# The opening's modulation as rows on TensorE in four column tiles, and the queries' rotation in two parts, in a two-layer retention, attention and gated-linear-attention block on one Trainium2 core

## The chip, the cores and the metric

One core of one Trainium2 chip runs the whole kernel. The metric is device time in microseconds (us), lower is better. Before the change the median of three runs is 1180.37 us (1178.66 to 1183.4). Engines are called as the profile calls them: PE (TensorE, with PEld for its weight loads), DVE (VectorE), ACT (ScalarE), POOL (GpSimd), SP (SyncE, which issues the DMAs). Names like L556 are line numbers of the kernel before.

## The reference, cut to what matters

```python
c_act = jax.nn.silu(c)
for l in range(2):                                    # DEPTH
    shift, scale, gate = split(c_act @ ada_w[l] + ada_b[l], 3)     # 1024 x 3072
    h = rms_norm(x, norm_w[l]) * (1 + scale) + shift
    proj = h @ w_in[l]
    # retention: rope(rq), rope(rk), rv, gate rz; 4 heads of 64, chunks of 64
    # mla: 8 heads, q = (rms_norm(q_lat) @ w_uq), 64 plain + 32 rotated columns
    #      k, v from kv_lat, masked softmax by chunks of 64
    # gla: 4 heads, gated linear attention
    mixed = concat(r_o * silu(rz), m_o * silu(mz), g_o * silu(gz))
    x = x + gate * (mixed @ w_out[l])
return rms_norm(x, final_norm)                        # x is 1024 x 1024, fp32
```

All is fp32. A product of two fp32 tiles is made by `mm3` (L556 to L558): both operands are split into a high and a low part of the type fp32r, and hi·hi, hi·lo and lo·hi are added in PSUM, so three matmuls for each pair of 128 x 128 weights and 512 tokens. A plain fp32 matmul shows as two passes in the trace.

## The kernel before, in words

The tokens lie along the free dimension, in two halves (hf) of 512; features lie on partitions, in eight tiles (KT = 8, index k) of 128. The order of instructions on each engine is the order of the program text. Beside the main stream of projections runs a list of tasks: Python generators that `tick()` advances. Each `yield n` in a task means "continue n ticks later", and a tick comes after each group of three matmuls of a projection. So a `yield` decides between which of the projections' matmuls a task's instructions stand on each engine.

**The opening** (`start`). The norm of x and the modulation of layer 0 must be there before the first projections. Shift and scale are columns of `ada_w[0]` times silu(c), 8 tiles of 128 columns each. `column(k)` makes tile k of both: the scale's on DVE (L301, a product with a replicated row of silu(c), summed along the free dimension), the shift's for k = 0 to 4 (SHIFT_PE = 5) on PE by eight fp32 matmuls of one column (L311), for k = 5 to 7 on DVE as well. `make(k)` then forms h of tile k for both halves: DVE `ht` (L347), ACT high part (L348, with the shift as its bias), DVE low part (L354). Between the second and the third stands `column(k + 1)`. The first three weights, rq1, rq2 and rk1 (their tiles are named ssq_wh, ada_wh and mkh_wh in the trace), are split into high and low by ACT (L456) and DVE (L457): the first ahead, the others after `make(0)` and `make(1)`. The table `behind` gives PE one weight's matmuls after `make(0)`, three groups after `make(1)` and five after `make(2)`; from k = 3 on all three weights' (18 matmuls). After k = 2 ACT makes the sines of the positions (`trig`, L406 to L410, with two loads of its table).

**The queries** (`mla_queries`). The rotated columns of the queries are made first: two tiles for each half (`qx`). After a tick, `q_rope` rotates both halves on DVE (L732 to L737, six operations of 128 x 512 each), splits them (cast on DVE L1118, rest on POOL L1119) and writes them to DRAM (qr). Then come eight tiles of the plain columns (four pairs of heads by two halves, trace name mq_pspj, 6 matmuls each), each emptied by `pair_out`: ACT high part L1106, DVE low part L1107, two writes. They go through two PSUM banks ("pj"). Retention's blocks run as a task beside this: scores (L790), DVE's masked scores `ram` (L793) and weighted keys `rks` (L804), the state (L802, L815, `rst` L825), values (L830, L834), then a norm (`hsq` L860 on ACT, its sum L862 on DVE).

**The maxima** (`mla_max`). Ahead of the softmax each head's scores are made once in one pass only to find row maxima: 12 units for each head, a matmul of 128 to 512 keys (L1243) and DVE's maximum (L1245), one unit per 1.15 ticks. q (qn and qr) and k are read back from DRAM. When a head's units are done, its close reduces (L1211), waits `yield 4`, and transposes the maxima on PE (L1215). The close of head h stands inside head h + 1, ahead of its third group of queries, and it is run inside the same generator, so its yield also moves all later units. Units that are left when the values' projection (mv, L1189) comes up are issued back to back ahead of it.

## Time and profile before

| what | value |
|---|---|
| median of three runs | 1180.37 us (1178.66 to 1183.4) |
| the profiled execution | 1183.94 us, its span 1182.2 us |
| mean granted clock of PE in it | 0.978 |
| PE / DVE / ACT / POOL busy | 95% / 66% / 50% / 44% of the span |
| DMA | 169.01 MB, mean 143 GB/s |

The span is the time from the first to the last instruction in the profiled execution, and all rows of the trace are placed in it by their start. A row of the timeline reads: start, duration, engine, line, operation, output<-inputs, shape, number of instructions put together, and in brackets how long the engine had been idle and what ended that. Durations of matmuls are modelled and overlap: the time of one in a dense stretch is the distance between two starts. In the table of windows each engine's busy time stands with the number of its instructions, then the granted clock (1.00 is full), the share of the DMA engines and their GB/s.

### The profile page before, as it was taken

How to read it: one execution, taken by the hardware profiler on the slowest of the kernel's cores; microseconds unless marked ns; L12 is line 12 of the kernel's file. 1: busy time of each engine (PE TensorE's matmuls, PEld its weight loads, DVE VectorE, ACT ScalarE, POOL GpSimd, SP SyncE). 2: the span in 40 equal slices, each digit the busy share in tenths (PEclk: the TensorE clock that was granted, in tenths of full speed). 3: DMA queues.
4: the chain of work that ended last, by engine and by line, in shares of the span. 5: the costliest groups of instructions: out<-in, count | busy, mean ns of one | idle time of the engine just before them, and what ended most of it. 6: DMA issues, size and time to landing. Idle time of an engine off the chain costs nothing.

```text
span 1182.2 us, 16973 instructions
## 1 busy us (share of the span) xinstructions
PE 1118.6 (95%) x5968; PEld 933.9 (79%) x5968; DVE 785.9 (66%) x1366; ACT 596.2 (50%) x1164; POOL 525.8 (44%) x459
## 2 busy tenths in 40 slices
PE   6999996899999999999999999969999999999996
PEld 3878985688878788887787898748888878888896
DVE  6866666568765656868875476474866565686754
ACT  6434342243554678863543434324355557886431
POOL 0055152445433446683565333335453344668620
PEclk8899998899999999999999999989999999999999
DMA  9725661662137534238443356155211653424722
GB/s 370 257 87 161 203 223 54 213 194 73 41 96 216 130 90 108 64 134 311 178 167 101 113 169 239 38 213 150 63 59 41 199 130 90 108 63 156 255 88 72
DMA packets 65585, 169.01 MB, mean 143 GB/s; under 512 B 10262, under 2 KB 13334, under 8 KB 65500
## 3 DMA queue, kind: packets, MB, share of 16 engines
q1 hardware_dynamic: 65500, 167.93, 44.8%
q8 instruction: 47, 0.77, 0.3%
q14 instruction: 38, 0.31, 0.1%
HBM read 125.36 MB, written 38.41 MB: 139 GB/s over the span
## 4 chain that ended last, share of the span: by engine, by line
PE 75%; DVE 12%; DMA 5%; ACT 4%; issue 3%; POOL 1%; SPq 0%; DVEq 0%; POOLq 0%; ACTq 0%
PE mhead_psacc L1294 3%; PE mhead_psacc L1292 3%; PE mhead_psacc L1293 3%; PE pmz_pspj L556 3%; PE pmz_pspj L557 2%; PE pmz_pspj L558 2%; DMA ada_aw<-awc 2%; DVE mmax_mx L1245 2%; PE wo_pss L558 2%; PE wo_pspj L556 2%; PE wo_pss L556 2%; PE wo_pss L557 2%; PE wo_pspj L558 2%; PE wo_pspj L557 2%; PE mhead_pss L1260 2%
## 5 line engine op out<-in xcount | busy, mean ns | idle before, releaser
L457 POOL TENSOR_TENSOR wwo_wl<-wwo_wst,wwo_wh 128x1024 fp32r<-128x1024 f32 x27 | 69.4, 2575 | 39.0 <-ACT wwo_wh L456 38.9
L1245 DVE TENSOR_REDUCE mmax_mx<-mmax_psmm 128x1 f32<-128x512 f32 (+1 forms) x96 | 57.4, 598 | 34.9 <-PE mmax_psmm L1243 33.9
L1269 POOL TENSOR_TENSOR mhead_wh<-mhead_p,mhead_wh 128x384 fp32r<-128x384 f32 (+1 forms) x48 | 57.9, 1207 | 45.5 <-DVE mhead_wh L1268 39.9
L576 DVE SCALAR_TENSOR_TENSOR ada_aw<-ada_aw,silrow 128x512 f32<-128x512 f32 x64 | 60.6, 966 | 18.6 <-DMA ada_aw<-awc 18.4
L1274 DVE TENSOR_TENSOR mhead_ph<-mhead_pss,mhead_ph 128x512 fp32r<-128x512 f32 x48 | 33.0, 688 | 36.2 <-ACT mhead_pss L1273 35.7
L556 PE MATMUL pmz_pspj<-mkh_h,wmz_wh 128*128 128x512 f32 x128 | 53.3, 417 | 0.0
L1269 POOL TENSOR_TENSOR mhead_wl<-mhead_p,mhead_wl 128x128 fp32r<-128x128 f32 (+1 forms) x48 | 35.8, 746 | 34.7 <-DVE mhead_wl L1268 34.7
L557 PE MATMUL pmz_pspj<-mkh_h,wmz_wh 128*128 128x512 f32 x128 | 50.9, 397 | 0.0
L558 PE MATMUL pmz_pspj<-mkh_h,wmz_wl 128*128 128x512 f32 x128 | 50.6, 395 | 0.0
L556 PE MATMUL mq_pspj<-latn_lat,wuq_wh 128*128 128x512 f32 x48 | 21.6, 450 | 26.0 <-DVE mq_pl L1107 25.6
L558 PE MATMUL wo_pspj<-gran_mx,wwo_wl 128*128 128x512 f32 (+1 forms) x120 | 44.3, 369 | 1.9 <-POOL wwo_wl L457 1.9
L556 PE MATMUL wo_pss<-gran_mx,wwo_wh 128*128 128x512 f32 (+1 forms) x120 | 44.5, 371 | 0.0
L556 PE MATMUL wo_pspj<-gran_mx,wwo_wh 128*128 128x512 f32 (+1 forms) x120 | 44.5, 371 | 0.0
L557 PE MATMUL wo_pss<-gran_mx,wwo_wh 128*128 128x512 f32 (+1 forms) x120 | 44.1, 368 | 0.0
L557 PE MATMUL wo_pspj<-gran_mx,wwo_wh 128*128 128x512 f32 (+1 forms) x120 | 44.1, 368 | 0.0
L558 PE MATMUL wo_pss<-gran_mx,wwo_wl 128*128 128x512 f32 (+1 forms) x120 | 44.1, 368 | 0.0
L457 POOL TENSOR_TENSOR wrk_wl<-wrk_wst,wrk_wh 128x1024 fp32r<-128x1024 f32 x3 | 8.0, 2682 | 79.5 <-ACT wrk_wh L456 79.5
L600 ACT ACTIVATE ssq_sq<-ssq_x 128x512 f32<-128x512 f32 (+1 forms) x31 | 16.6, 534 | 50.9 <-DVE ssq_x L1371 50.9
L605 DVE TENSOR_TENSOR ssq_sq<-ssq_sq,ssq_sq 128x512 f32<-128x512 f32 (+1 forms) x30 | 30.9, 1029 | 13.6 <-ACT ssq_sq L600 13.6
L1272 ACT ACTIVATE mhead_ph<-mhead_pss 128x512 fp32r<-128x512 f32 x48 | 28.6, 596 | 17.8 <-PE mhead_pss L1262 17.3
L1243 PE MATMUL mmax_psmm<-mmax_mxk,mmax_mxq 104*128 104x512 f32 (+1 forms) x96 | 35.5, 370 | 2.0 <-DVE mmax_mx L1245 1.5
L556 PE MATMUL pv_pspj<-wgv_wh,mkh_h 128*128 128x256 f32 x128 | 37.0, 289 | 0.0
(560 smaller groups left out, 4124.7 us busy)
## 6 DMA issues: line engine op xcount, KB each, us to landing
ada_aw<-awc SPq DMA_DIRECT2D x64, 256.0 KB
wwo_wst<-wo SPq DMA_DIRECT2D x32, 512.0 KB
aw<-awc SPq DMA_DIRECT2D x11, 512.0 KB
x<-xT SPq DMA_DIRECT2D x8, 512.0 KB
kn<-mk_ph SPq DMA_DIRECT2D x16, 256.0 KB
kn<-mk_pl SPq DMA_DIRECT2D x16, 256.0 KB
qn<-mq_ph SPq DMA_DIRECT2D x16, 256.0 KB
qn<-mq_pl SPq DMA_DIRECT2D x16, 256.0 KB
```

Source lines behind the costliest of these rows:

```text
L457: (eng or nc.gpsimd).tensor_tensor(lo, src, hi.bitcast(F32), ALU.subtract)
L556: mm(ps, lh, rh, start=start, stop=False)
L557: mm(ps, lh, rl, start=False, stop=False)
L558: self.last = mm(ps, ll, rh, start=False, stop=stop)
L576: step = nc.vector.scalar_tensor_tensor(v, v, 1.0, self.silrow[:, cs], ALU.mult, ALU.mult, accum_out=t[:, 2 * j + i:2 * j + i + 1])
L1243: nc.tensor.matmul(ps[:, :w], st["q"][0:104, 128 * i:128 * i + 128], st["k"][0:104, 512 * j:512 * j + w], start=True, stop=True)
L1245: nc.vector.tensor_reduce(mx[:, i, j:j + 1], ps[:, :w], AX.X, ALU.max)
L1269: nc.gpsimd.tensor_tensor(pl, p, ph.bitcast(F32), ALU.subtract)
L1274: nc.vector.tensor_tensor(pl, s, ph.bitcast(F32), ALU.subtract)
L1292: mm(acc[:, o], vh, ph, start=(j == 0), stop=False, skip_group_check=True)
L1293: mm(acc[0:64, o], vl, ph, start=False, stop=False, skip_group_check=True)
L1294: mm(acc[:, o], vh, pl, start=False, stop=last, skip_group_check=True)
```

## The change

It has four parts.

1. **The opening's first half as columns, its second half as rows.** Columns 0 to 3 stay with `column(k)`: shift of k = 0 on PE, all other sums on DVE. Columns 4 to 7 of shift and scale are made as two rows of 512 on PE: `row(1)` after k = 1 and `row(3)` after k = 2. Each is eight fp32 matmuls of 32 x 512 with silu(c), repeated 32 times, as the stationary operand, four at a time in the four column tiles of the array (`tile_position` (0, 32j)), which leaves four partial sums at 32 partitions each. ACT copies the bank, and after rq1's matmuls of the next k `row_out` turns the row into four columns: four matmuls of one column with a selector that adds the four partial sums, and DVE writes them into `mod` (`ada_out`). The weights' loads and splits for all three names come ahead of the columns; `behind` is gone, so each k does its 18 matmuls at once; `trig` stands after k = 3.
2. **The queries' rotation** of half 0 stands right behind that half's two tiles, that of half 1 behind the eight plain tiles.
3. **`yield 4` in the maxima's close is `yield 7`.**
4. Two inputs are laid out for the rows (`awk`, a 0/1 selector column `sel`). The bytes loaded in the opening stay sixteen tiles of 512 KB.

```diff
-SHIFT_PE = 5
...
-    A["aws"] = ada_w[0][:, :128 * SHIFT_PE].reshape(KT, 128, SHIFT_PE, 128).transpose(2, 1, 0, 3).reshape(SHIFT_PE, 128, D)
+    A["aws"] = ada_w[0][:, :128].reshape(KT, 128, 128).transpose(1, 0, 2).reshape(128, D)
+    A["awk"] = ada_w[0].reshape(4, 2, 128, 6, 512)[:, :, :, 1:4:2].transpose(3, 0, 2, 1, 4).reshape(2, 4, 128, 1024)
...
                 dma(pos, A["pos"])
         names = ("rq1", "rq2", "rk1")
         wst, aw = {}, {}
-        for k in range(KT):
-            if k < len(names):
-                wst[names[k]] = self.sl(name="wst")
-                dma(wst[names[k]], A["wi"][0, MIDX[names[k]]])
+        for n in names:
+            wst[n] = self.sl(name="wst")
+            dma(wst[n], A["wi"][0, MIDX[n]])
+        for k in range(4):
             aw[k] = [self.sl(name="aw") for _ in range(2)]
-            dma(aw[k][1], A["awc"][2 + k // 4, k % 4])
-            dma(aw[k][0], A["aws"][k] if k < SHIFT_PE else A["awc"][k // 4, k % 4])
+            dma(aw[k][1], A["awc"][2, k])
+            dma(aw[k][0], A["awc"][0, k] if k else A["aws"])
+        for ch in (1, 3):
+            aw["row", ch] = [self.sl(name="aw") for _ in range(4)]
+            for i in range(4):
+                dma(aw["row", ch][i], A["awk"][ch // 2, i])
         self.ahead()
         V.memset(self.ones, 1.0)
         V.memset(self.eps, EPS)
...
         ssq = [self.ps("acc") for _ in range(2)]
         o = VO["c"]
         self.silu(self.silc, self.vec[:, o:o + KT], self.sm([128, KT]), self.sm([128, KT]))
+        silrep = self.pt((128, KT, 32), name="silrep")
+        V.tensor_copy(silrep, self.silc.unsqueeze(2).to_broadcast([128, KT, 32]))
         ab = self.sm([128, KT])
         o = VO["adab"]
         V.tensor_scalar(ab, self.vec[:, o + KT:o + 2 * KT], 1.0, None, ALU.add)
...
             V.scalar_tensor_tensor(self.mod[0][2 + ch][:, j], t[:, 1:2], ab[:, k:k + 1], self.vec[:, o:o + 1],
                                    ALU.add, ALU.mult)
             src = t[:, 0:1]
-            if k < SHIFT_PE:
+            if k == 0:
                 ps = self.ps()
                 for i in range(KT):
                     nc.tensor.matmul(ps[:, 0:1], aw[k][0][:, 128 * i:128 * i + 128], self.silc[:, i:i + 1],
...
                 along(0)
             o = VO["adab"] + k
             nc.scalar.activation(self.mod[0][ch][:, j], src, AF.Identity, bias=self.vec[:, o:o + 1])
-        w_split("rq1")
+
+        def row(ch):
+
+            self.lab = "ada_"
+            ps, r = self.ps(), self.pt(name="row")
+            for i in range(KT):
+                g = slice(32 * (i % 4), 32 * (i % 4) + 32)
+                nc.tensor.matmul(ps[g, :], silrep[:, i, :], aw["row", ch][i // 2][:, 512 * (i % 2):512 * (i % 2) + 512],
+                                 start=(i < 4), stop=(i >= 4), tile_position=(0, g.start))
+            nc.scalar.copy(r, ps)
+            return r
+
+        def row_out(ch, r):
+
+            self.lab = "ada_"
+            ps = self.ps()
+            for j in range(4):
+                nc.tensor.matmul(ps[:, j:j + 1], r[:, 128 * j:128 * j + 128], self.vcol("sel", 0),
+                                 start=(j == 0), stop=True, skip_group_check=True)
+            self.ada_out(0, ch, ps)
+        for n in names:
+            w_split(n)
         self.lab = "rstd_"
         ys, zs = [self.pt(name="y") for _ in range(2)], [self.pt(name="rt") for _ in range(2)]
         for hf in range(2):
...
                 g = self.h[k][hf] = self.sl((128, 2, 512), F32R, "h")
                 V.scalar_tensor_tensor(ts[hf], self.x[k][:, hs[hf]], a, ys[hf], ALU.mult, ALU.mult)
                 nc.scalar.activation(g[:, 0, :], ts[hf], AF.Identity, bias=b)
-            if 0 < k < KT - 1:
+            if 0 < k < 3:
                 column(k + 1)
             self.lab = "mkh_"
             for hf in range(2):
...
             if k == 0:
                 column(1)
             return last
-        behind = {0: (("rq1", 0),), 1: (("rq1", 1), ("rq2", 0), ("rq2", 1)),
-                  2: (("rq1", 2), ("rq2", 2), ("rk1", 0), ("rk1", 1), ("rk1", 2))}
+        rows = {}
         for k in range(KT):
             self.start_last = make(k)
-            if k < 2:
-                w_split(names[k + 1])
-            for n, i in behind.get(k, [(n, k) for n in names]):
-                mm(n, i)
-            if k == 2:
+            for n in names:
+                mm(n, k)
+                if (k, n) == (2, "rq1"):
+                    row_out(1, rows[1])
+                if (k, n) == (3, "rq1"):
+                    row_out(3, rows[3])
+            if k in (1, 2):
+                rows[2 * k - 1] = row(2 * k - 1)
+            if k == 3:
                 self.trig(ang, kk, s)
         for n, o, r in (("r", 0, 32), ("m", 32, 16)):
             self.tab[n] = []
...
                 self.uq_mtile(w, ql, i, hf, ps)
                 x[hf].append(self.pt(name="qx"))
                 nc.scalar.copy(x[hf][i], ps)
+            if hf == 0:
+                self.q_rope(l, x[hf], hf, *tab[hf])
+                self.lab = "mq_"
         yield
-        for hf in range(2):
-            self.q_rope(l, x[hf], hf, *tab[hf])
         self.lab = "mq_"
         for pr in range(4):
             for hf in range(2):
                 ps = self.ps("pj")
                 self.uq_mtile(wn, ql, pr, hf, ps)
                 self.pair_out(self.qn[l], pr, hf, ps)
+        self.q_rope(l, x[1], 1, *tab[1])
 
     def mla_keys(self, l, kvl):
         (wh, wl), = self.weight((l, "ukvk"))
...
             self.lab = "mmax_"
             m8 = self.sm([128, 8])
             nc.vector.tensor_reduce(m8, mx, AX.X, ALU.max)
-            yield 4
+            yield 7
             self.lab = "mmax_"
             ps = self.ps()
             nc.tensor.matmul(ps[0:8, 0:128], m8, self.cst("ident"), start=True, stop=True)
```

How the order moves, at the three places that the prediction speaks of.

DVE at the queries' third plain tile, before. mq_pl is the low part that frees the bank (1856 is the first half's eviction that the third tile waits for), mrope and mq_qx the rotation of half 1 from its second operation, retc retention's block, hnorm its norm:

```order
L733 TENSOR_TENSOR mrope_rb_1785<-mq_qx_1570,pv_tab_1323 128x512
L736 TENSOR_TENSOR mq_qx_1610<-mq_qx_1610,pv_tab_1322 128x512
L734 TENSOR_TENSOR mq_qx_1570<-mq_qx_1570,pv_tab_1322 128x512
L737 TENSOR_TENSOR mq_qx_1610<-mq_qx_1610,mrope_rb_1785 128x512
L735 TENSOR_TENSOR mq_qx_1570<-mq_qx_1570,mrope_ra_1784 128x512
L1118 CAST mrope_qrh_1792<-mq_qx_1570 128x512
L1118 CAST mrope_qrh_1798<-mq_qx_1610 128x512
L793 TENSOR_TENSOR retc_ram_1817<-retc_pss_1811,cst 128x2x128
L793 TENSOR_TENSOR retc_ram_1817<-retc_pss_1812,cst 128x2x128
L804 TENSOR_TENSOR retc_rks_1826<-retc_psmm_1823,cst 128x256
L862 TENSOR_REDUCE hnorm_sm_1845<-hnorm_hsq_1843 128x8
L1107 TENSOR_TENSOR mq_pl_1856<-mq_pspj_1804,mq_ph_1855 128x512
```

The same place after, from the output gate's zu of the projection ahead of it (mq_pl_1821 is the same eviction):

```order
L463 SCALAR_TENSOR_TENSOR prz_zu_1762<-mq_rz_324_1617,prz_zt_1761 128x512
L823 TENSOR_TENSOR retc_ram_1782<-retc_pss_1776,cst 128x2x128
L823 TENSOR_TENSOR retc_ram_1782<-retc_pss_1777,cst 128x2x128
L834 TENSOR_TENSOR retc_rks_1791<-retc_psmm_1788,cst 128x256
L855 SCALAR_TENSOR_TENSOR mq_rst_1515<-mq_rst_1517,cst,retc_psmm_1793 64x64 x2
L855 SCALAR_TENSOR_TENSOR mq_rst_1516<-mq_rst_1518,cst,retc_psmm_1793 64x64 x2
L892 TENSOR_REDUCE hnorm_sm_1810<-hnorm_hsq_1808 128x8
L1139 TENSOR_TENSOR mq_pl_1821<-mq_pspj_1769,mq_ph_1820 128x512
```

The sixteen operations of the rotation (eight for each half) are gone from between the second tile and its eviction. They stand now, half 0 first, ahead of the second block of retention, whose masked scores are ram_1590:

```order
L762 TENSOR_TENSOR mrope_ra_1548<-mq_qx_1546,pv_tab_1308 128x512
L763 TENSOR_TENSOR mrope_rb_1549<-mq_qx_1537,pv_tab_1308 128x512
L766 TENSOR_TENSOR mq_qx_1546<-mq_qx_1546,pv_tab_1307 128x512
L764 TENSOR_TENSOR mq_qx_1537<-mq_qx_1537,pv_tab_1307 128x512
L767 TENSOR_TENSOR mq_qx_1546<-mq_qx_1546,mrope_rb_1549 128x512
L765 TENSOR_TENSOR mq_qx_1537<-mq_qx_1537,mrope_ra_1548 128x512
L853 COPY mq_rst_1517<-retc_psmm_1601 64x64 x2
L853 COPY mq_rst_1518<-retc_psmm_1601 64x64 x2
L1150 CAST mrope_qrh_1556<-mq_qx_1537 128x512
L1150 CAST mrope_qrh_1562<-mq_qx_1546 128x512
L823 TENSOR_TENSOR retc_ram_1590<-retc_pss_1584,cst 128x2x128
L823 TENSOR_TENSOR retc_ram_1590<-retc_pss_1585,cst 128x2x128
```

Six operations and two casts have come between the first block's rks and the second block's ram.

PE where the maxima end and the values' projection mv begins, before:

```order
L558 MATMUL pmz_pspj_3744<-mkh_h_590,wmz_wl_3562 128x512
L1243 MATMUL mmax_psmm_3854<-mmax_mxk_2243,mmax_mxq_2242 128x384
L1243 MATMUL mmax_pss_3857<-mmax_mxk_2243,mmax_mxq_2242 128x512
L1243 MATMUL mmax_psmm_3860<-mmax_mxk_2243,mmax_mxq_2242 128x512
L1243 MATMUL mmax_pss_3863<-mmax_mxk_2243,mmax_mxq_2242 128x128
L1243 MATMUL mmax_psmm_3866<-mmax_mxk_2243,mmax_mxq_2242 128x512
L1243 MATMUL mmax_pss_3869<-mmax_mxk_2243,mmax_mxq_2242 128x256
L1243 MATMUL mmax_psmm_3872<-mmax_mxk_2243,mmax_mxq_2242 128x512
L1243 MATMUL mmax_pss_3875<-mmax_mxk_2243,mmax_mxq_2242 128x384
L1243 MATMUL mmax_psmm_3878<-mmax_mxk_2243,mmax_mxq_2242 128x512
L1243 MATMUL mmax_pss_3881<-mmax_mxk_2243,mmax_mxq_2242 128x512
L556 MATMUL mv_pspj_3894<-wukvv_wh_3676,pmz_lat_3556 128x256
```

The same after, its last units (the twelve rows ahead of these are ten units of head 6 and the first two of head 7):

```order
L1247 MATMUL mmax_psmm_3834<-cst,mmax_sm_3832 8x128
L1275 MATMUL mmax_psmm_3839<-mmax_mxk_2228,mmax_mxq_2227 128x384
L1275 MATMUL mmax_pss_3842<-mmax_mxk_2228,mmax_mxq_2227 128x512
L1275 MATMUL mmax_psmm_3845<-mmax_mxk_2228,mmax_mxq_2227 128x512
L1275 MATMUL mmax_pss_3848<-mmax_mxk_2228,mmax_mxq_2227 128x128
L1275 MATMUL mmax_psmm_3851<-mmax_mxk_2228,mmax_mxq_2227 128x512
L1275 MATMUL mmax_pss_3854<-mmax_mxk_2228,mmax_mxq_2227 128x256
L1275 MATMUL mmax_psmm_3857<-mmax_mxk_2228,mmax_mxq_2227 128x512
L1275 MATMUL mmax_pss_3860<-mmax_mxk_2228,mmax_mxq_2227 128x384
L1275 MATMUL mmax_psmm_3863<-mmax_mxk_2228,mmax_mxq_2227 128x512
L1275 MATMUL mmax_pss_3866<-mmax_mxk_2228,mmax_mxq_2227 128x512
L586 MATMUL mv_pspj_3879<-wukvv_wh_3621,pmz_lat_3516 128x256
```

Ten units stood ahead of mv in one piece; now it is 22 units and a transposition (L1247).

In the opening the copy of each row stands on ACT ahead of the next k's high parts, and the table loads of the sines behind those of k = 3; before, they stood behind those of k = 2.

More of the change, by code (lines that the diff above doesn't have):

```diff
@@ L147, in host_layout @@
         np.concatenate([gla_norm, gla_norm], 1).T, final_norm.reshape(KT, 128).T, INV,
-        c[0].reshape(KT, 128).T], 1)
+        c[0].reshape(KT, 128).T, (np.arange(128) % 32 == 0)[:, None].astype(f)], 1)
     A["cst"] = CST
@@ L157 @@
 for _n, _w in (("normw", DEPTH * 8), ("adab", DEPTH * 24), ("qn", DEPTH * 2), ("kvn", DEPTH),
-               ("gb2", DEPTH), ("gln", DEPTH), ("fin", 8), ("inv", 1), ("c", 8)):
+               ("gb2", DEPTH), ("gln", DEPTH), ("fin", 8), ("inv", 1), ("c", 8), ("sel", 1)):
     VO[_n] = _o
```

## The prediction

> **What bounds the kernel now.** I read the page first (busy time, then the chain that ended last), then TensorE's waits by releaser, and then the timeline around the largest wait. These are the page's rows of TensorE's busy time and of the chain:
>
> ```profile
> PE 1118.6 (95%) x5968; PEld 933.9 (79%) x5968; DVE 785.9 (66%) x1366; ACT 596.2 (50%) x1164; POOL 525.8 (44%) x459
> PE 75%; DVE 12%; DMA 5%; ACT 4%; issue 3%; POOL 1%; SPq 0%; DVEq 0%; POOLq 0%; ACTq 0%
> ```
>
> TensorE (PE) is the bound: some 64 us of the span of 1182.2 are not busy. So a change pays only where it ends a wait of TensorE, takes instructions off it, or raises its clock. Its waits, in us in total, times, longest:
>
> ```profile
> PE mq_pspj L556 <- DVE mq_pl L1107: 25.6, 4, 12.5
> PE mmax_psmm L1215 <- DVE mmax_sm L1211: 3.7, 3, 2.1
> ```
>
> The first is two stalls of 12.5 us, one per layer, and two short ones. TensorE's timeline in layer 0, then layer 1 (start, us; the brackets hold the idle time before the row):
>
> ```profile
> 197.21 0.40 PE L558 MATMUL mq_pspj<-latn_lat,wuq_wl 128*128 128x512 f32 x1
> 210.13 0.80 PE L556 MATMUL mq_pspj<-latn_lat,wuq_wh 128*128 128x512 f32 x1 [12.53 <-DVE mq_pl L1107]
> 778.07 0.79 PE L556 MATMUL mq_pspj<-latn_lat,wuq_wh 128*128 128x512 f32 x1 [12.53 <-DVE mq_pl L1107]
> ```
>
> The third tile of the queries' non-rotated half needs the PSUM bank that L1107 empties. VectorE (DVE), GpSimd (POOL) and ScalarE (ACT) around it:
>
> ```profile
> 195.30 0.68 DVE L732 TENSOR_TENSOR mrope_ra<-mq_qx,pv_tab 128x512 f32<-128x512 f32 x1
> 201.15 1.75 DVE L732 TENSOR_TENSOR mrope_ra<-mq_qx,pv_tab 128x512 f32<-128x512 f32 x1
> 207.01 0.76 DVE L1118 CAST mrope_qrh<-mq_qx 128x512 fp32r<-128x512 f32 x2
> 208.81 0.68 DVE L862 TENSOR_REDUCE hnorm_sm<-hnorm_hsq 128x8 f32<-128x512 f32 x1
> 209.40 1.28 DVE L1107 TENSOR_TENSOR mq_pl<-mq_pspj,mq_ph 128x512 fp32r<-128x512 f32 x2
> 201.04 2.97 POOL L1119 TENSOR_TENSOR mrope_qrl<-mq_qx,mrope_qrh 128x512 fp32r<-128x512 f32 x2 [3.31 <-DVE mrope_qrh L1118]
> 206.49 0.63 ACT L860 ACTIVATE hnorm_hsq<-retc_ho 128x512 f32<-128x512 f32 x1 [9.87 <-DVE mq_qx L737]
> ```
>
> VectorE works on the rotation of both halves from 195.30 to 207.8 (two of its operations at 1.75 instead of 0.68 while GpSimd runs beside them), and the eviction of the second tile stands behind that in its queue. The stall is VectorE's order, not its load.
>
> It costs more than its length, since the granted clock falls. Four windows: the start of the stall, its end with what follows, and the same around the longest wait of L1215.
>
> ```profile
> 197.39:200.80 3.41, 0.22 (x1) 1.00 0.00 0
> 200.80:214.50 13.70, 4.37 (x10) 0.50 0.60 230
> 344.17:347.58 3.41, 1.32 (x7) 1.00 0.71 243
> 347.58:351.00 3.42, 3.42 (x9) 0.51 0.54 179
> ```
>
> The ten matmuls after the stall take 4.37 us, 0.44 each; at the full clock such a matmul takes 0.23 (worked out from a window in the part on the opening). That is 2.1 us in layer 0. In layer 1 the slow stretch is three matmuls shorter: I take 1.5.
>
> **The queries' rotation in two parts.** It removes nothing; it moves one half of the rotation (six operations, two casts, two GpSimd subtractions and four writes) to behind the first two tiles, and the other half to behind the eighth. At the third tile VectorE now has, after prz_zu's 0.69, only the ram, rks and rst operations of one retention block (0.76 + 0.41 + 1.22), the 0.68 reduction and the eviction (0.64). With ScalarE's hsq no longer held for 9.87, they end by my count near 199.1, so tile three starts 11.0 earlier than at 210.13: −11.0 and the clock's −2.1 in layer 0, −11.0 and −1.5 in layer 1.
>
> What is late next? The first half now stands ahead of ram and rks of retention's second block: six operations at 0.61 and two casts, 4.4 us, or 6.5 if two are slowed to 1.75 again. TensorE has this row as work between that block's scores and values:
>
> ```profile
> 182.14 0.48 PE L556 MATMUL prz_pspj<-mkh_h,wrz_wh 128*128 128x512 f32 x1
> ```
>
> The values' operands must be there just before it, at about 181.7; I find the last one, GpSimd's, ready near 182.5. The second half does the same ahead of retention's last block. I take 0.6 for each, between 0 and 2.5 (a slowed half not covered at all). Net: −13.1 + 1.2 = −11.9 in layer 0, −12.5 + 1.2 = −11.3 in layer 1, together **−23.2**.
>
> The second half's result is written later. VectorE would start it near 215, end near 219 to 224, and GpSimd and the write end near 229. The readers are the maxima's loads and first unit:
>
> ```profile
> 233.46 0.51 SPq L1147 DMA_DIRECT2D mmax_mxq<-qn  x1
> 237.96 0.45 SPq L1151 DMA_DIRECT2D mmax_mxk<-kn  x1
> L1243 PE MATMUL mmax_psmm<-mmax_mxk,mmax_mxq x3: 226/338/459, 251.7 to 255.2; 104*128 104x128 f32 x1, 104*128 104x384 f32 x1, 104*128 104x512 f32 x1
> ```
>
> With the stall gone, 251.7 becomes 238.5, and the loads (233.5 to 238.4 before, 5 us) then run from about 229.5 to 234. That leaves some 4 to 5 us; I cost it at nothing.
>
> **`yield 4` to `yield 7`.** Each head's transposition comes three steps later. That removes the waits at L1215 (−3.7 over both layers) and the half clock behind the longest (seven matmuls and two maxima in 3.42 us, 3.42 − 9 × 0.23 = 1.4 too long). In return all later units slide back by three steps per head. Before, ten maxima were left to stand back to back ahead of the values' projection (mv); now 22 and a transposition are:
>
> ```profile
> 400.67 0.34 PE L1243 MATMUL mmax_psmm<-mmax_mxk,mmax_mxq 104*128 104x384 f32 x1
> 404.32 0.28 PE L556 MATMUL mv_pspj<-wukvv_wh,pmz_lat 128*128 128x256 f32 x1
> 402.12 0.68 DVE L1245 TENSOR_REDUCE mmax_mx<-mmax_psmm 128x1 f32<-128x512 f32 x1
> 402.72 0.28 DVE L1245 TENSOR_REDUCE mmax_mx<-mmax_pss 128x1 f32<-128x128 f32 x1
> 402.92 0.68 DVE L1245 TENSOR_REDUCE mmax_mx<-mmax_psmm 128x1 f32<-128x512 f32 x1
> ```
>
> Back to back they go at VectorE's pitch: 0.60 from start to start for 512 columns, 0.20 for 128, and in proportion 0.33 for 256 and 0.47 for 384. A whole head (six of 512, two of each other size) is 5.6 us, the ten units 5.1, of which TensorE saw 404.32 − 400.67 = 3.65, as two banks run ahead. 22 units are 5.1 + 5.6 = 10.7, less the two in flight about 9.9: +6.25. The 12 units that left the stream took about 0.2 each beside other work there: −2.4. Other VectorE work in between: +0.5. That is +4.4 per layer, +8.8 over both; with −3.7 and −1.4, **+3.7**. Bounds: −4 (the earlier stream wins back all of it) to +12 (the clock halves in the drain, where TensorE would be about 38% busy; the window at 344.17 with 1.32 of 3.41 busy was followed by a half clock).
>
> The row first: a wait of 2.09 us at L1215 was followed by a clock of 0.51 from 347.58 to 351.00. The Trainium skill (TensorE: Matmul & The Clock Gate, Part 1, "What's actually happening") says that the clock halves after an idle window of about 3.4 us, one that runs freely. Read as a fully idle window, that rule leaves the clock whole here, so the change would have 1.4 less to gain and the drain would never be slowed; the trace speaks against that reading, and I keep both terms.
>
> **The opening.** TensorE's clock and busy time before and after the clock rises, a column sum on TensorE at either clock, and what the other engines pay:
>
> ```profile
> 26.76:40.41 13.65, 11.95 (x35) 0.50 1.03 417
> 40.41:74.00 33.59, 32.77 (x159) 1.00 0.45 137
> 35.35 0.79 PE L557 MATMUL ada_pspj<-mkh_h,ssq_wh 128*128 128x512 f32 x1 [0.46 <-DVE mkh_h L354]
> 30.85 3.40 PE L311 MATMUL ada_psmm<-silc,aw 128*128 128x1 f32 x16
> 41.65 1.84 PE L311 MATMUL ada_psmm<-silc,aw 128*128 128x1 f32 x16
> 33.15 1.22 DVE L301 SCALAR_TENSOR_TENSOR aw<-aw,silrow 128x1024 f32<-128x1024 f32 x1
> 43.79 1.28 ACT L406 ACT_TABLE_LOAD   x1
> 48.75 1.32 ACT L348 ACTIVATE mkh_h<-mkh_ht,mod 128x512 fp32r<-128x512 f32 x2
> ```
>
> The full clock's matmul: the second window's 159 instructions are 32 passes of two column sums (1.84 each) and 127 matmuls, (32.77 − 3.68)/127 = 0.23. Off TensorE go three column sums (3.4 at the half clock, 1.84 twice): −7.1. On it come two rows of 8 fp32 matmuls, 16 passes, and two row_outs (8 passes, about 0.9 each). An fp32 pass of 512 columns is 0.43: (102.10 − 101.01 − 0.23)/2 from these rows, where two passes and one 0.23 matmul (the line left out) stand ahead of the second:
>
> ```profile
> 101.01 1.02 PE L609 MATMUL rstd_psmm<-latn_lss,ones 128*128 128x512 f32 x2
> ...
> 102.10 0.39 PE L557 MATMUL pmq_pspj<-mkh_h,wmq_wh 128*128 128x512 f32 x1
> ```
>
> Let R be the time of a row. I walked the new order through: k=0's 18 matmuls end near 34.7 (the clock rises some 5 us after 28.55, as it did, at 40.41, after the gap before 35.35); k=1 waits about 1.7 for VectorE, which now makes both sums of columns 1 and 2 (2.5 us a column) ahead of the low part, and ends near 40.3; row one; k=2 waits 2.0 (its h stands behind the row's 0.6 copy on ScalarE) and ends, with a row_out of 0.9, near 47.1 + R; row two; k=3 likewise near 53.9 + 2R; the trigonometry (43.79 to 48.75, 4.96 us of ScalarE) is now ahead of k=4, which waits 0.7 and ends near 59.2 + 2R; k=5 to 7, with no column left to make, are 54 matmuls at 0.227, and end at 71.4 + 2R, against 74.0 now. The sum is −2.6 + 2R. The bounds of R: 6.88 (16 × 0.43, one after the other) and 1.72 (four at once). The nearest row is retention's pairs on half the array's rows, eight matmuls in 187.07 − 186.43 = 0.64, where the same width and number on the full array would be 8 × 0.11 (L815: four in 0.45) = 0.9:
>
> ```profile
> 186.43 0.72 PE L790 MATMUL retc_pss<-prk_rh,prk_rh 64*128 64x128 f32 x8
> 187.07 0.44 PE L802 MATMUL retc_psmm<-cst,prk_rh 128*128 128x128 f32 x2
> 187.34 0.61 PE L815 MATMUL retc_psmm<-pv_v,retc_rks 128*128 128x128 f32 x4
> ```
>
> Tiles of the array do run beside each other there. I take 1.72: **+0.9**, with ends −1 and +11.2.
>
> The Trainium skill (the same page, Part 3) gives 2.38 times for three column tiles at 512 columns, and TensorEngine Tiling (Array Packing), "Key Properties", says that a change of the tiling mode drains the engine. An estimate from the former, 6.88/2.38 = 2.9, would make this term +3.2. No run here shows column tiles yet.
>
> The first weights' loads go ahead of the column tiles, same bytes. They are landed before the 26.59 at which TensorE starts, and what starts it is ScalarE's h, so I cost that at nothing; should the first column tile come late, each tile is about 1.25 us.
>
> **The sum.** +0.9 − 23.2 + 3.7 = −18.6 on the profiled execution (1183.94, its span 1182.2): 1165.3. That execution is 3.6 over the median of 1180.37. From the median I forecast 1161.8. About 0.5%, 5.9 us, is what a measurement of this kernel can tell from no change.
>
> **The rivals.**
> - *The drain is free* (the values' projection or the heads would have waited anyway, and the heads start no later): then the maxima give −5.1 and not +3.7, in all 1153. For it: VectorE empties mv's banks too, so mv may wait for it either way. Against: the units' pitch is VectorE's own. 0.2.
> - *The rows run one after another*: +11.2 for the opening, in all 1172. For it: the fp32 operands need two passes each, and L790 gained only a third of the full width's time. Against: that gain is there. The change then does not do what it says. 0.12.
> - *The stall comes back at retention*: the half rotation ahead of ram and rks, slowed by GpSimd (1.75 for 0.68), costs 3 to 4 us four times: 1174. Against: it needs all four waits at the far end of the bound above. 0.08.
> - *Slower*: last tile, second half of the rotation, write, load, first maximum. If VectorE reaches that half 17 us later than I count (behind retention and the output gate in its queue), the first maxima stand 12 us late in TensorE's order and hold all behind them; both stalls return there, with the drain and the rows on top: +5, 1185. It begins at 5 us late and decides at 17. Against: the eviction of the eighth tile leaves VectorE nearly idle. 0.05.
>
> **How the numbers follow.** My forecast has 0.55. The range of 1151 to 1174 takes in the free drain and the serial rows, and leaves out the slower case and half of the returned stall. Faster by over 0.5% (under 1174.5): 0.55 + 0.2 + 0.11 + 0.04 = 0.9; I give 0.87 as some of the slow ends add up, 0.08 for the same and 0.05 for slower.
>
> **What the profile after would show.** Right: no wait over 1 us at the third query tile in either layer and a clock of 1.0 there; no row of L1215's successor waiting for its reduction; 22 maxima and a transposition in about 10 us ahead of mv; the opening's last matmul near 75; a row near 1.7 us. Wrong: a wait over 2 us at retention's values or scores, or at the first maximum; a clock of 0.5 in the drain; a row of near 7 us; a gap of over 2 us at k=1.

## The result, and the profile after

The changed kernel takes 1191.98 us (median of ten runs, 1188.75 to 1198.02) against 1181.56 of the kernel before (ten runs, 1178.66 to 1186.07): ratio 1.0086, 95% interval 1.0069 to 1.0103. It is 10.4 us slower. The forecast was 1161.8, with a range of 1151 to 1174; the result lies outside it. The profiled execution has a span of 1187.0, the shortest of the ten; so the trace shows 4.8 us of the loss against the profiled execution before, and the rest is between executions, whose mean granted clock goes from 0.978 (1188.75 us) to 0.970 (1198.02 us).

The busiest engine and TensorE's largest waits after:

```profile
PE 1125.4 (95%) x5952; PEld 935.4 (79%) x5952; DVE 794.0 (67%) x1358; ACT 596.0 (50%) x1162; POOL 530.0 (45%) x459
```

```profile
PE mmax_psmm L1275 <- DVE mmax_mx L1277: 5.4, 5, 2.3
...
PE ada_pspj L586 <- ACT mkh_h L375: 4.7, 3, 2.0
PE mmax_psmm L1247 <- DVE mmax_sm L1243: 4.0, 2, 2.0
PE mq_pspj L586 <- DVE mq_pl L1139: 3.7, 4, 1.6
PE glac_psacc L1039 <- DVE mmax_mx L1277: 3.4, 2, 1.7
```

The waits of 25.6 us at mq_pl have become 3.7. That is most of them, though the third tile still waits 1.6, where the forecast had no wait over 1. New are waits of TensorE for the maxima's reductions on VectorE, at the units (L1275), at a transposition (L1247) and at gla's blocks (L1039). Placed along the program, by the start of the same TensorE instruction in the two traces:

| from the span's start to the start of | before | after | difference | since the row above |
|---|---|---|---|---|
| the second block of projections (prk) | 73.96 | 76.94 | +2.98 | +2.98 |
| retention's norm (hout), layer 0 | 243.69 | 237.15 | −6.54 | −9.5 |
| gla's output gate (pgz) | 288.39 | 286.27 | −2.12 | +4.4 |
| the values' projection (mv) | 404.32 | 406.79 | +2.47 | +4.6 |
| the second layer's projections (prq) | 607.34 | 609.70 | +2.36 | −0.1 |
| hout, layer 1 | 811.05 | 803.56 | −7.49 | −9.9 |
| pgz, layer 1 | 854.42 | 851.44 | −2.98 | +4.5 |
| mv, layer 1 | 966.65 | 971.91 | +5.26 | +8.2 |

**Beside gla's preparation** (between hout and pgz) the forecast had no cost. TensorE's and VectorE's timeline after:

```profile
278.73 0.50 PE L1275 MATMUL mmax_pss<-mmax_mxk,mmax_mxq 104*128 104x512 f32 x1 [1.15 <-DVE mmax_mx L1277]
...
282.27 0.47 PE L1275 MATMUL mmax_psmm<-mmax_mxk,mmax_mxq 104*128 104x128 f32 x1 [2.32 <-DVE mmax_mx L1277]
```

```profile
276.52 1.70 DVE L969 TENSOR_TENSOR glap_gkp<-pgk_gk,glap_gz 64x512 f32<-64x512 f32 x2
278.25 0.42 DVE L1277 TENSOR_REDUCE mmax_mx<-mmax_pss 128x1 f32<-128x256 f32 x1
278.71 0.93 DVE L960 TENSOR_TENSOR glap_gkm<-pgk_gk,glap_gel 128x256 f32<-128x256 f32 x1
...
280.65 0.84 DVE L965 TENSOR_TENSOR glap_gka<-pgk_gk,glap_gt 64x256 f32<-64x256 f32 x2
281.52 0.69 DVE L1277 TENSOR_REDUCE mmax_mx<-mmax_psmm 128x1 f32<-128x512 f32 x1
```

VectorE is at gla's products from 276.5 to 281.5 (called the burst), with one reduction between them; five units' reductions stand behind. Two units wait 1.15 and 2.32 us for a PSUM bank, and all projections stand behind them on TensorE. Three of the five units had been issued by the time the burst began (at 274.63, 275.57 and 276.47). Before the change it was two of four (at 281.85 and 282.79). The head's last unit was issued at 285.31, so the pause of its close fell on the burst, and no unit waited there over 0.7 us. TensorE's and VectorE's rows before:

```profile
281.85 0.40 PE L1243 MATMUL mmax_psmm<-mmax_mxk,mmax_mxq 104*128 104x512 f32 x1
...
285.31 0.38 PE L1243 MATMUL mmax_pss<-mmax_mxk,mmax_mxq 104*128 104x256 f32 x1
```

```profile
282.96 1.71 DVE L939 TENSOR_TENSOR glap_gkp<-pgk_gk,glap_gz 64x512 f32<-64x512 f32 x2
...
287.99 0.69 DVE L1245 TENSOR_REDUCE mmax_mx<-mmax_psmm 128x1 f32<-128x512 f32 x1
```

**In the drain** ahead of mv, the first unit, the last one ahead of the transposition, the transposition and mv:

```profile
395.14 0.34 PE L1275 MATMUL mmax_psmm<-mmax_mxk,mmax_mxq 104*128 104x384 f32 x1
...
399.51 0.38 PE L1275 MATMUL mmax_pss<-mmax_mxk,mmax_mxq 104*128 104x256 f32 x1
401.92 0.60 PE L1247 MATMUL mmax_psmm<-cst,mmax_sm 128*8 128x128 f32 x2 [2.02 <-DVE mmax_sm L1243]
...
406.79 0.42 PE L586 MATMUL mv_pspj<-wukvv_wh,pmz_lat 128*128 128x256 f32 x1
```

TensorE's windows (us, busy, clock): around the opening's second row, at gla's preparation, in the drain.

```profile
50.10:53.60 3.50, 1.88 (x10) 1.00 0.01 2
53.60:57.00 3.40, 3.40 (x14) 0.50 0.00 0
275.40:278.80 3.40, 2.25 (x18) 1.00 0.00 0
278.80:282.30 3.50, 1.18 (x8) 1.00 0.44 118
398.40:401.80 3.40, 1.26 (x4) 0.99 0.81 199
401.80:408.60 6.80, 6.67 (x21) 0.50 0.45 98
```

The drain takes 406.79 − 395.14 = 11.65 instead of 3.65, +8.0. The transposition of head 6 stands behind the first two units of head 7. The reduction that it waits for is the last in VectorE's queue, so TensorE runs dry for 2.0 us; then VectorE in turn has nothing to do for 1.31, until the first unit behind the transposition:

```profile
403.17 0.56 DVE L1277 TENSOR_REDUCE mmax_mx<-mmax_psmm 128x1 f32<-128x384 f32 x1 [1.31 <-PE mmax_psmm L1275]
```

The clock is halved for the rest of the drain and the first of mv. In layer 1 the drain takes 11.65 too (960.26 to 971.91), with the clock halved from 964.96 on.

**The opening.** The row is as forecast, but TensorE waits behind it:

```profile
39.41 1.92 PE L331 MATMUL ada_psmm<-aw,silrep 128*32 128x512 f32 x16
42.66 0.49 PE L586 MATMUL ada_pspj<-mkh_h,ssq_wh 128*128 128x512 f32 x1 [1.32 <-ACT mkh_h L375]
```

The copy of the row stands ahead of the next k's high part on ScalarE. After the second row the clock is halved from 53.6 to 60.4.

### The profile page after: what moved, and what is told of

It is laid out like the page before. It is cut to its first block, busy times and chain, and to the rows that moved or that the text cites. A ratio compares the mean times of both kernels' runs of the same rounds, so it can differ in the third digit from the quotient of the medians.

```text
span 1187.0 us, 16937 instructions
## 1 busy us (share of the span) xinstructions
PE 1125.4 (95%) x5952; PEld 935.4 (79%) x5952; DVE 794.0 (67%) x1358; ACT 596.0 (50%) x1162; POOL 530.0 (45%) x459
## 4 chain that ended last, share of the span: by engine, by line
PE 72%; DVE 14%; DMA 5%; ACT 4%; issue 4%; POOL 1%; SPq 0%; DVEq 0%; ACTq 0%; POOLq 0%
PE mhead_psacc L1326 3%; PE mhead_psacc L1324 3%; PE mhead_psacc L1325 3%; PE pmz_pspj L586 2%; PE pmz_pspj L587 2%; PE pmz_pspj L588 2%; DMA ada_aw<-awc 2%; DVE mmax_mx L1277 2%; DVE ada_aw L606 2%; PE wo_pss L588 2%; PE wo_pss L586 2%; PE wo_pss L587 2%; PE wo_pspj L586 2%; PE wo_pspj L588 2%; PE wo_pspj L587 2%
## 5 line engine op out<-in xcount | busy, mean ns | idle before, releaser
L606 DVE SCALAR_TENSOR_TENSOR ada_aw<-ada_aw,silrow 128x512 f32<-128x512 f32 x64 | 64.9, 1033 | 16.9 <-DMA ada_aw<-awc 16.8
L1275 PE MATMUL mmax_psmm<-mmax_mxk,mmax_mxq 104*128 104x512 f32 (+1 forms) x96 | 38.8, 406 | 6.2 <-DVE mmax_mx L1277 5.4
L1277 DVE TENSOR_REDUCE mmax_mx<-mmax_pss 128x1 f32<-128x256 f32 (+2 forms) x72 | 36.5, 506 | 6.2 <-PE mmax_pss L1275 5.5
```

The costliest lines, as they stand in the source:

```text
L606: step = nc.vector.scalar_tensor_tensor(v, v, 1.0, self.silrow[:, cs], ALU.mult, ALU.mult, accum_out=t[:, 2 * j + i:2 * j + i + 1])
L1275: nc.tensor.matmul(ps[:, :w], st["q"][0:104, 128 * i:128 * i + 128], st["k"][0:104, 512 * j:512 * j + w], start=True, stop=True)
L1277: nc.vector.tensor_reduce(mx[:, i, j:j + 1], ps[:, :w], AX.X, ALU.max)
```

## The experiments

The theory from these rows: the loss lies in `yield 7`, which slides the units (called the slide). The rival: the waits come from the rotation's split, since the maxima start earlier and VectorE has its second half late.

**1. The changed kernel with yield 4** (e1), **before with yield 7 alone** (e2), **with the rotation alone** (e3), **with the opening alone** (e4).

```diff
 # e1: in the changed kernel's close
-            yield 7
+            yield 4
 # e2: in the kernel before
-            yield 4
+            yield 7
 # e3: in the kernel before, the rotation's lines of the change
 # e4: in the kernel before, the opening's lines of the change
```

> The changed kernel with yield 4 in place of 7. Slide theory: the loss comes from the three ticks more in each head's close, which slide all later maxima units. In the changed kernel's trace that costs about 4.7 us a layer where gla's preparation keeps VectorE busy (units wait up to 2.3 us for their banks) and 8 us a layer in the drain ahead of mv, and wins back some 3.4. Taken away, the time is near 1165 (17 under before), without a wait over 1 us at L1275 beside gla's preparation and with ten units in the drain. Rotation theory: the waits at gla's preparation come from the rotation's split (maxima start 6.5 us earlier, VectorE has the second half late), so they stay and the time is near 1175.

> The kernel before with yield 7 alone. Slide theory: about 16 us slower than before (1195 to 1200), waits of 1 to 2.3 us at the maxima's units beside gla's preparation in both layers, 22 units in the drain, and a half clock in one or both drains. Rotation theory: about 4 us slower, no such waits beside gla's preparation.

> The kernel before with the rotation in two parts alone. Slide theory: 19 us faster (two stalls of 12.5 us and their half clock gone, about 1.7 us a layer given back at retention), 1162, no long waits at the maxima beside gla's preparation. Rotation theory: 10 us faster only, 1171, with those waits.

> The kernel before with the opening's part alone. All theories: within 4 us of before. A row takes 1.9 us and TensorE waits 1.3 us after each for ScalarE; if the clock then falls to a half for two windows as in the changed kernel's trace (53.6 to 60.4 us) the opening ends 3 us later than before, if not about 0.5 us earlier.

| | median, us | before, us | ratio, 95% |
|---|---|---|---|
| e1, yield 4 | 1170.86 | 1180.67 | 0.9909 (0.9878 to 0.9939) |
| e2, yield 7 alone | 1205.69 | 1180.67 | 1.0205 (1.0177 to 1.0234) |
| e3, rotation alone | 1163.37 | 1180.67 | 0.9841 (0.9811 to 0.9871) |
| e4, opening alone | 1187.55 | 1180.67 | 1.0062 (1.0037 to 1.0088) |

e1 lies between the 1165 of the slide theory and the 1175 of its rival; it holds the opening too, which costs more than was expected of it (e4). Yield 7 alone costs 25.0 us, more than the slide theory's 16; taken out of the changed kernel it gives 21.1 (1191.98 − 1170.86). The rotation alone gives 17.3, and its trace has no wait over 0.5 us at a unit: the rival falls. e4 is 6.9 slower, over the 4 expected, though its trace shows only 2.9 us of it (the opening, up to prk, ends at 75.57, that of e3 at 72.62). One trace against one says little here: the opening as it was before ends between 70.21 and 73.96 in the eight traces that have it (mean 72.3), the changed one between 75.57 and 78.17 in four (mean 77.1). The three parts add up to +14.6 for the +10.4 of the whole. In e3, TensorE's waits between 165 and 233 us:

```profile
PE mq_pspj L556 <- DVE mq_pl L1109: 1.8, 2, 1.6
PE retc_pss L790 <- DVE retc_ram L793: 1.4, 1, 1.4
PE prz_pspj L556 <- DVE mq_pl L1109: 1.2, 1, 1.2
...
```

**2. Only the first close, only the later closes.** Both on e3.

```diff
-            yield 4
+            yield 7 if h == 0 else 4      # e7
+            yield 4 if h == 0 else 7      # e13
```

> The kernel before with the rotation in two parts and yield 7 in the first head's close alone. The drain keeps its ten units. Slide theory: the three ticks put the units of the second head behind VectorE's burst at gla's preparation, 4.6 us a layer: 1172 to 1173, with waits of 1 to 2.3 us at the units there. Rival (all of the cost is in the drain): 1163 to 1165.

> The kernel before with the rotation in two parts, yield 4 in the first head's close and 7 in all later ones. The units beside gla's preparation stand where they stood; 18 units and a transposition are left for the drain. If yield 7 has two separate costs, the one beside gla's preparation (4 to 5 us a layer) is gone and the drain's is there: eight units more at VectorE's 0.2 to 0.6 are some 4 us, the half clock 1 to 2, less 3 us for units and waits gone from the stream, 2 to 4 us a layer: 1167 to 1171. If the two are one (the later heads' units meet VectorE's work elsewhere in the same way), waits over 1 us at units show in other stages and the time is over 1175.

e7: 1168.77, ratio 0.9881 (0.9854 to 0.9908); e13: 1170.98, ratio 0.9901 (0.9880 to 0.9923). Against e3's 1163.37 that is +5.4 and +7.6. e13 is as expected, e7 between its two expectations. e7's waits, at the same two units and as long as in the changed kernel:

```profile
275.36 0.50 PE L1245 MATMUL mmax_pss<-mmax_mxk,mmax_mxq 104*128 104x512 f32 x1 [1.16 <-DVE mmax_mx L1247]
278.90 0.33 PE L1245 MATMUL mmax_psmm<-mmax_mxk,mmax_mxq 104*128 104x128 f32 x1 [2.32 <-DVE mmax_mx L1247]
```

By the traces the stretch from hout to pgz is 4.5 and 4.8 us longer than e3's in the two layers; behind it 3.9 and 1.2 come back, where the waits at the transpositions are gone. The drain of ten units, now with a transposition, takes 4.08 instead of 3.65. In e13 the waits beside gla's preparation are gone, and the drain, with 19 units by the trace, has the transposition's wait inside it:

```profile
394.38 0.38 PE L1217 MATMUL mmax_psmm<-cst,mmax_sm 128*8 128x128 f32 x2 [2.02 <-DVE mmax_sm L1213]
```

It takes 9.50 in layer 0, where the transposition comes ahead of the half clock (from 395.89) and VectorE idles 0.85 behind it, and 9.96 in layer 1, where it comes inside the half clock (from 948.85) and VectorE idles 1.31. So 0.46 of such a drain is the half clock's.

e13 is not the drain alone: in layer 0 one unit waits 3.95 (at 347.54) behind VectorE's sums for the next layer's modulation (L576), a third place. From hout to mv e13 is 4.9 longer than e3 in layer 0 and 3.3 in layer 1, which has no such wait.

Together e7 and e13 make 13.0 of yield 7's 21 to 25. Of the rest, e2's drain of 22 units is some 2 us a layer longer than e13's (+8.0 against +5.9 and +6.3, by the traces). TensorE also waits 1.7 us in each layer at gla's blocks (1.68 in the changed kernel, 1.71 in e2), and not in e7 or e13. And both e7 and e13 win the transposition's wait of 2.08 that stands in e3's layer 0, which can be won only once.

**3. The close as a task of its own**, so that the pause holds only the transposition (the step of `yield MAXW` behind the close goes too): in the changed kernel (e5) and on e3 with yield 4 (e6).

```diff
                     if i == 2 and done:
-                        yield from close(*done)
+                        self.task(close(*done), 0)
                         done = None
-                        yield MAXW
```

> The changed kernel, yield 7 kept, but each close runs as a task of its own, so the pause holds the transposition back and no longer the units. Slide theory: the pause costs only because the units behind it stand still. No unit is left for the drain, the time falls by 20 to 26 us under the changed kernel, to between 1165 and 1172. Rival: the late transposition itself (its PSUM bank, its reduction) costs the time; then it stays near 1190.

> The kernel before with the rotation in two parts and each close (yield 4) as a task of its own. Slide theory: the ten units that stand back to back ahead of mv go into the stream, 3.65 us become about 2, in each layer, so 3 us under the rotation alone: 1160. If units that come earlier meet VectorE's burst at gla's preparation instead, waits over 1 us at the units appear there and the time is 1163 to 1170.

e5: 1182.88 (before 1181.34), ratio 1.0013 (0.9996 to 1.0029), 9 us under the changed kernel instead of 20 to 26. e6: 1188.23, ratio 1.0046 (1.0028 to 1.0063): 25 us slower than the rotation alone. Both expectations missed. With no pause the drain is gone, but the units come so densely in the stream that VectorE does not follow. TensorE's waits in e6 fit that:

```profile
PE mv_pspj L556 <- DVE pmz_vl L1191: 7.2, 2, 3.6
PE mmax_psmm L1217 <- DVE mmax_mx L1246: 7.1, 4, 1.9
...
PE glac_psacc L1009 <- DVE mmax_mx L1246: 4.2, 4, 1.5
```

So "the pause costs" falls as a theory. My reading of e6, e7 and e13 together is that the pause is VectorE's time to catch up, and that it matters whether it falls on VectorE's burst, and how many units are left behind it; no run tests that by itself.

**4. The transposition alone later** (e10, on e3), **and yield 5** (e12, on e3).

```diff
             yield 4
+            self.task(turn(h, m8), 3)     # e10: the rest of close, three ticks later
```

> The kernel before with the rotation in two parts; the close still holds the units for 4 ticks, but the transposition comes 3 ticks later still, as a task of its own. The units stand where they stood, so nothing slides; if the pause of the units is what matters for the bound of VectorE and the late transposition is harmless, the waits at the transposition (3.7 us) and the half clock behind the longest (1.4) go: 1158 to 1160 against 1163 with the rotation alone. If the late transposition costs by itself (its bank, the order on ScalarE), 1163 or more.

> The kernel before with the rotation in two parts and yield 5. Ten units and a transposition are left for the drain. One tick more in the first close moves the second head's units a third of the way to where yield 7 put them: if the cost beside gla's preparation grows evenly, 1.5 us a layer, less 1 to 2 us of waits at the transposition, 1164 to 1166; if it is a step that only comes when the units cross VectorE's burst, 1161 to 1163.

e10: 1163.32 (before 1181.99), ratio 0.9844 (0.9822 to 0.9866): no gain over e3, where 3 to 5 us were expected if the late transposition does no harm. Its waits at the transpositions moved; they now stand beside gla's preparation, for a bank behind the units' reductions:

```profile
263.62 0.39 PE L1220 MATMUL mmax_psmm<-cst,mmax_sm 128*8 128x128 f32 x2 [2.58 <-DVE mmax_mx L1252]
```

e12: 1161.06, ratio 0.9823 (0.9800 to 0.9847), at the better end of what was expected, and no clear difference from e3's 0.9841.

**5. The rows earlier** (e8, on e1), **and on one column tile** (e9, on e8).

```diff
 # e8: each row behind rq1's matmuls of its k
-            if k in (1, 2):
+                if k in (1, 2) and n == "rq1":
                     rows[2 * k - 1] = row(2 * k - 1)
 # e9: all eight matmuls of a row at the first tile
-                nc.tensor.matmul(ps[g, :], silrep[:, i, :], aw["row", ch][i // 2][:, 512 * (i % 2):512 * (i % 2) + 512],
-                                 start=(i < 4), stop=(i >= 4), tile_position=(0, g.start))
+                nc.tensor.matmul(ps[0:32, :], silrep[:, i, :], aw["row", ch][i // 2][:, 512 * (i % 2):512 * (i % 2) + 512],
+                                 start=(i == 0), stop=(i == KT - 1), tile_position=(0, 0))
 # ... the row's copy and the selector's matmuls then take these 32 partitions alone
```

> The changed kernel with yield 4, and each row's matmuls behind rq1's of the same k instead of behind rk1's. If TensorE's 1.3 us behind each row come from the row's copy, which stands ahead of the next k's high part on ScalarE, both waits go: 3 us under the same kernel with late rows, 1167 to 1168. If the high part is late for another reason, or the half clock after the rows is what costs, no change: 1171.

> The changed kernel with yield 4 and early rows, each row's eight matmuls on one column tile instead of four. If the four tiles run beside each other, a row's 16 passes go from 1.92 us to 6.9 (16 x 0.43), and the opening ends some 10 us later than with four tiles, near 80. If a matmul with 32 stationary columns is itself quicker, a row stays near 1.9.

e8: 1163.72 (before 1181.34), ratio 0.9841 (0.9808 to 0.9874), 7 us under e1, where 3 were expected. Its opening ends at 70.36; e1's at 78.17, with the clock halved for 6.8 us in it (53.98 to 60.80), e4's at 75.57 without that. Against the rotation alone (e3, 1163.37) there is no gain. No wait follows the row: rq2's matmuls run on while ScalarE copies it.

```profile
36.83 1.92 PE L331 MATMUL ada_psmm<-aw,silrep 128*32 128x512 f32 x16
38.69 0.50 PE L586 MATMUL ada_pss<-mkh_h,ada_wh 128*128 128x512 f32 x1
```

e9, with one tile: 1171.26, ratio 0.9919 (0.9894 to 0.9944), the opening 10.6 us longer:

```profile
36.98 7.05 PE L330 MATMUL ada_psmm<-aw,silrep 128*32 128x512 f32 x16
```

16 passes take 7.05 on one column tile and 1.92 on four: the tiles do run beside each other.

**6. Combinations**: e8 with the late transposition (e11), e8 with yield 5 (e14).

> Early rows, rotation in two parts, units held for 4 ticks and the transposition 3 ticks later: the same 3 to 5 us under the kernel without the late transposition (1164), so 1159 to 1161; the early rows give another 2 us only where no half clock takes them back.

> Early rows, the rotation in two parts, yield 5. If the opening with early rows is 2 us shorter than before's and yield 5 2 us better than 4, both add to the rotation's gain: 1159 to 1161. If the half clock takes back the opening's gain, as in the run with early rows and yield 4: 1161 to 1164.

e11: 1166.17, ratio 0.9868 (0.9846 to 0.9891), a miss: here too a transposition and units wait beside gla's preparation (2.2 and 2.1 us at the longest). e14: 1161.38 (before 1182.27), ratio 0.9824 (0.9804 to 0.9844). Like e12 it is 1.8% under the kernel before, and some 2.6% under the changed one. Which of the two is better these runs don't tell, so they show no gain from the early rows beside the rotation's.

## Why the prediction was wrong

- **The rotation, −23.2.** Right in kind: 17.3 us (15.2 to 22.3 by the interval), 9.5 and 9.6 a layer by e3's trace for 11.9 and 11.3. The third tile still waits 1.6: it starts at 199.55 in e3, which is 1.3 ahead there, so 1.8 later than my 199.1. Retention takes 2.2 in layer 0 (1.4 at the second block's scores, 0.4 twice at its last values) for my 1.2: two operations of the first half run beside GpSimd's split of the gate's weights and take 2.5 and 2.9 us, longer than the 1.75 that I allowed for. VectorE's and GpSimd's rows in e3:

```profile
169.68 2.48 DVE L732 TENSOR_TENSOR mrope_ra<-mq_qx,pv_tab 128x512 f32<-128x512 f32 x1 [0.80 <-ACT mq_qx L1078]
...
173.29 2.86 DVE L734 TENSOR_TENSOR mq_qx<-mq_qx,pv_tab 128x512 f32<-128x512 f32 x1
```

```profile
169.22 2.39 POOL L457 TENSOR_TENSOR wrz_wl<-wrz_wst,wrz_wh 128x1024 fp32r<-128x1024 f32 x1
172.80 2.80 POOL L457 TENSOR_TENSOR wrz_wl<-wrz_wst,wrz_wh 128x1024 fp32r<-128x1024 f32 x1 [1.19 <-ACT wrz_wh L456]
```

- **yield 7, +3.7: this is the step that failed**, at 21 to 25 us. By the traces of before and after, both layers together, it splits like this:

| | forecast | traces |
|---|---|---|
| beside gla's preparation (hout to pgz) | 0 | +8.93 |
| from pgz to the drain | −9.9 | −3.17 |
| the drain | +13.5 | +16.00 |
| sum | +3.6 (rounded to +3.7 there) | +21.76 |

The first row is the place that was missing. I took "all later units slide back" as a question of the drain alone and never asked beside which of VectorE's work they would come to stand. At gla's preparation it is 4.4 to 5 us a layer; e7 shows it nearly by itself. The second row was 2 × 2.4 for the units gone from the stream, 3.7 for the waits at L1215 and 1.4 for the clock. The units were near: in e13's layer 1 nine units gone give 3.05, of which 0.80 is a transposition's wait. But new waits came into that stretch in the changed kernel: 1.68 at gla's blocks in each layer, 1.29 at L904 in layer 0 (357.52) and, in layer 1, a half clock of 3.4 us (from 883.04) that before's trace does not have. In the third row "Back to back they go at VectorE's pitch" was right, but I counted the 22 units as one queue: the transposition inside it lets TensorE wait 2.0 us and then VectorE 1.31, so +8.0 a layer for my 6.25 + 0.5.

- **The opening, +0.9.** The row's time was right (1.92 for 1.72) and the rival of serial rows is out (7.05). The end was near as well: 71.4 + 2 × 1.72 is 74.8, and e4's trace has 75.57. But I compared it with the 74.0 of a single trace, the latest of the eight with the old opening (mean 72.3), and had no half clock behind the second row, which three of the four traces with the changed opening have; these three end at 76.94 to 78.17. The means are 4.8 apart, and alone the part measured 6.9 (4.4 to 10.4). e8 shows that the waits behind the row's copy, which I priced but took as unavoidable, can go.
- **The clock.** The half clock in the drain was in the range (+12 for the maxima), not in the value. The clock fell in each of the six drains profiled with 19 or 22 units, but it makes only some 0.5 of such a drain (e13). The prediction's doubt about a wholly idle window as the condition holds: 1.26 and 1.18 us of work in a window were followed by a half clock.
- **The rivals.** *The drain is free* is out (+8.0). *Slower* came true by another mechanism: no first maximum was late (its lead of 6.55 us over before is that of hout). The range missed because it took yield 7's worst case as +12, a clock in the drain, and had no bound for a burst elsewhere.

## What to carry to other kernels

A delay in a generator moves everything behind it on every engine: list which instructions each moved one comes to stand behind, all along the program, and not only where it ends. If a unit of work needs more time on a second engine than on the bound one, count the second engine's backlog; a pause may be what keeps it short. A stage that differs from one execution to the next is compared by several traces: the same old opening ended anywhere from 70.21 to 73.96. Put a producer's matmuls one group earlier when the next group's operand is queued behind its eviction.

## What the runs showed of the hardware

- Four column tiles of 32: 16 fp32 passes of 512 columns in 1.92 us against 7.05 on one tile, 3.7 times.
- The clock fell after windows of about 3.4 us with 1.18, 1.26 and 1.88 us of matmuls: TensorE need not be idle throughout. How busy the window is does not decide it alone: in the same trace one with 2.73 (961.55 to 964.96) was followed by a half clock too, and those with 1.76 (313.02 to 316.43) and 2.25 (275.4 to 278.8) were not.
- With GpSimd at a weight split, two VectorE operations of 128 x 512 on SBUF took 2.5 and 2.9 us instead of 0.68.
